# Transposes in lasting PSUM banks, an ordered opening, an output tail in halves, and TensorE in program order through the second attention

## The chip, the cores and the metric

The kernel runs on one core of a Trainium2 chip. The metric is the time of one execution on the device in microseconds (us); the median of several runs is given. Engines are called as in the profile: PE is TensorE's matmuls, PEld its weight loads, DVE VectorE, ACT ScalarE, POOL GpSimd, SP the engine that issues most DMAs.

## The reference

A two-layer encoder step over 2048 prompt frames and 64 sample frames, width 1024, 16 heads of 64, all in float32. Shortened:

```python
# layer 0: chunk-band softmax attention (own chunk of 64 and 8 before it)
q, k, v, gate = split(rms_norm(x, norm_a) @ w_in_a, 4)
p = softmax(q @ k.T * SCALE + rel_bias[clip(rel)] masked to the band)
x = x + ((p @ v) * silu(gate)) @ w_out_a
# keys and values shared by the second layer, from the new x
kb, vb = split(rms_norm(x, norm_kv) @ w_kv, 2)
# layer 1: stick-breaking attention, strictly causal
q, gate = split(rms_norm(x, norm_b) @ w_in_b, 2)
z = q @ kb.T * SCALE
log_fail = where(mask, log_sigmoid(-z), 0)
w = where(mask, exp(log_sigmoid(z) + (sum of log_fail over later keys)), 0)
x = x + ((w @ vb) * silu(gate)) @ w_out_b
y = rms_norm(x, norm_f)
```

The sample frames attend to cached keys as well (512 rows in layer 0, 2048 in layer 1). The outputs are y for both groups and the new rows of keys and values.

## The kernel before

Each float32 factor is kept as two parts, a rounded one (names ending in h) and the rest (ending in l), and a product is the sum of three matmuls (hh, hl, lh). `split` makes the two parts: a copy on ACT, a subtraction on DVE.

There are four stages. **Projections a** (0 to about 727 us): for 17 tiles of 128 frames, `normed` loads a tile (`xt`), takes its squares on ACT (`junk`), the root on POOL (`rstd`), scales it, transposes it on PE into a two-bank PSUM tile (`ps_tr`) and splits it into `x_own` or `big`; values are projected (`ps_v`) with weights `vwh`/`vwl`, made block by block from `vraw` in two halves of the columns. Then keys, queries and gates are projected by `jobs` (`ps_t`) with weights `wh`/`wl`, with `stages` between them that rearrange caches. **First attention** (to about 1323 us), with its output projection (`ps_o`) until 1431 us. **Projections b** (to 2040 us) is the same code on the new x. **Second attention** follows (scores from 2059 to 3201 us), and its last output tiles until 3307 us.

[...] Before, each stage opens its own PSUM pool: in the projections five banks `mm`, two `tr`, one `nat`; in the first attention four for scores `z`, one for sums `acc`, three `wt`; in the second two `z`, two `acc`, one constant (`own`) and three `wt`. The `wt` banks take the transposes of weights and also the accumulation of projections that run beside the attention (`ps_j`, deferred projections, and `ps_o`).

An attention is a list of beats, written out by `Beat`. In the second attention a beat takes one tile of 128 queries against one chunk of up to 512 keys: two score matmuls; f is the sigmoid on ACT; `two` multiplies pairs on POOL; a scan on DVE over `two`; POOL fills the odd places (`s`). On the diagonal (chunk of the queries themselves) the scan takes f directly and widths are 128, 256, 384 and 512. A pack of four tiles' weights is transposed later (`turn`: four 128x128 transposes into a `wt` bank, then the split into `ph` on ACT and `pl` on DVE), and two beats (HOLD) after that multiplied with the values (`products`: sums `acc<-ph,vt` and `acc<-pl,vt`). LAG is the number of beats from an item's last scores to its first `turn`. Heads come in 8 pairs; the frames in two parts (groups of 512 queries 1, 0, then 3, 2), and each pair ends with two or three beats of the sample (`qs`). Key and value chunks have four buffers each. Beside this, `step` takes two of a projection's eight depth blocks (six matmuls) at a rate of 0.3 a beat. `end` drains what is left.

The order of instructions on each engine is chosen at build time: the builder schedules the program by its own timing model, except for instructions that are told to keep the program's order. `InOrder` marks these: in the version before only steps wrapped by `in_place` (loads and splits of projections beside the attention), once `order.amid` is set. On the chip each engine runs its list in order and waits on semaphores.

The output tile (`out_tile`) loads the gated result (`og`) and the residual (`xr`), splits the first into `oh`/`ol` (two buffers each), does 48 matmuls in two halves of columns (the sample's 32), and adds. `finish` then calls `done_b`: squares of 1024 columns on ACT, `rstd` on POOL, one scaling on DVE with the norm's weights `gf`, one DMA. The sample's tile is the last.

Of the kernel before, what the change touches and what calls it, by code (L numbers as in the profile page):

```python
# [9 lines left out]
F32 = mybir.dt.float32  # L10
# [34 lines left out]
LAG = dict(a=2, b=5)  # L45
# [28 lines left out]
class InOrder:  # L74


    def __init__(self, tc):

        self.tc, self.on, self.amid = tc, False, False

    def engine(self, engine):
        outer = self

        class Engine:
            def __getattr__(self, name):
                op = getattr(engine, name)

                def traced(*args, **kwargs):
                    ins = op(*args, **kwargs)  # L89
# [10 lines left out]
def encoder_step(ctx: ExitStack, tc: tile.TileContext, a: dict, o: dict):  # L100
    nc = tc.nc
    order = InOrder(tc)
    dve, act, gps, pe = (order.engine(x) for x in (nc.vector, nc.scalar, nc.gpsimd, nc.tensor))
# [21 lines left out]
    opool = ctx.enter_context(tc.tile_pool(name="out", bufs=1))  # L125

# [79 lines left out]
    def projections(L, x_of, begin, w_v, cv, gv, out_v, jobs, first, prompt, sample, stages):  # L206
        with (
# [7 lines left out]
            with tc.tile_pool(name=f"v_{L}", bufs=2) as pool:  # L215
# [3 lines left out]
                def normed(t, scale=gps.tensor_scalar):  # L219
                    r0, n = TOK[t]  # L220
                    xt = pool.tile([P, D], F32, name="xt", tag="xt", bufs=3)
# [14 lines left out]

                seq = [t for gs_ in ORDER for g in gs_ for t in range(4 * g, 4 * g + 4)] + [len(TOK) - 1]
                if L == "a":
                    seq.sort()
                normed(seq[0], dve.tensor_scalar)  # L240
                begin()
                for half in range(2):
                    wh, wl = [], []
                    for k in range(NK):
                        raw = pool.tile([P, CH], F32, name="vraw", tag="vraw", bufs=2)
                        c = cv + half * CH
                        nc.sync.dma_start(raw, w_v[k * P : (k + 1) * P, c : c + CH])
                        h_ = pool.tile([P, CH], F32R, name="vwh", tag=f"vwh{k}", bufs=1)
                        l_ = pool.tile([P, CH], F32R, name="vwl", tag=f"vwl{k}", bufs=1)
                        act.activation(h_, raw, AF.Copy, scale=gv[:, k : k + 1])  # L250
                        dve.scalar_tensor_tensor(
                            l_, raw, gv[:, k : k + 1], f32(h_), ALU.mult, ALU.subtract
                        )
                        wh.append(h_)
                        wl.append(l_)
                    for i, t in enumerate(seq):
                        r0, n = TOK[t]
                        if half == 0 and i + 1 < len(TOK):
                            normed(seq[i + 1])
# [29 lines left out]
                        if dst is not None:  # L289
                            vn = pool.tile([P, CH], F32, name="vn", tag="vn", bufs=2)  # L290
                            act.activation(vn[:n], out, AF.Copy)
# [6 lines left out]
            with tc.tile_pool(name=f"st_{L}", bufs=5) as spool, tc.tile_pool(name=f"t_{L}", bufs=2) as pool:  # L298
                for j, (kind, w, c0, g) in enumerate(jobs):
                    for hp in range(HP):  # L300
                        for _ in range(-(-len(stages) // (len(jobs) * HP - j * HP - hp))):
                            stages.pop(0)(pool, psum)
# [4 lines left out]
                        nc.scalar.dma_start(raw, w[:, c : c + P].rearrange("(k p) c -> p k c", p=P))  # L307
                        wh = opool.tile([P, NK, P], F32R, name="wh", tag="oh", bufs=2)
                        wl = opool.tile([P, NK, P], F32R, name="wl", tag="ol", bufs=2)
                        scaled_split(wh, wl, raw, g)  # L310
                        for hf, (r0, n, chunks) in enumerate(HALVES):
# [27 lines left out]
                            if kind == "k":  # L339

                                cols = slice(hp * P, hp * P + P)
                                for c in range(0, HALF, CH):
                                    b = hf * HALF + c - first
                                    if b >= 0:
# [3 lines left out]
                                        natural(pool, psum, kf, 0, P, 4, prompt[b : b + CH, cols])  # L348
                                if hf == 0:
# [3 lines left out]
                                    natural(pool, psum, kf, 0, NS, 1, sample[:, cols])  # L353
# [3 lines left out]
    def stage_cache(L, hp, c, pool, psum):  # L357
# [4 lines left out]
        ps = psum.tile([P, CH], F32, name="ps_c", tag="tr", bufs=1)  # L362
# [21 lines left out]
    def stage_diff(where, t, half, pool, psum):  # L384
# [28 lines left out]
    def stage_bias(hp, pool, psum):  # L413
# [13 lines left out]
    def natural(pool, psum, kf, at, n, nt, dst):  # L427
        ps = psum.tile([P, 4, P], F32, name="ps_n", tag="nat", bufs=1)
# [124 lines left out]
    def weigh(pool, psum, acc, blocks, first, last, along=None):  # L553
# [4 lines left out]
        def turn():  # L558
            if along:
                along()  # L560
            wt = psum.tile([P, CH], F32, name="wt", tag="wt", bufs=banks["wt"])
# [26 lines left out]
    def weigh_sample(pool, psum, acc, blocks, first, last):  # L588
# [3 lines left out]
        def turn():  # L592
            wt = psum.tile([P, CH], F32, name="wt", tag="wt", bufs=banks["wt"])
# [51 lines left out]
    def job_steps(L, jobs, x2, psum, first, prompt):  # L645

        return [
            late_job(L, *job, hp, x2, psum, first, prompt)
# [5 lines left out]
    def late_job(L, kind, w, c0, g, hp, x2, psum, first, prompt):  # L654
# [13 lines left out]
        def some(c, k0):  # L668
            if k0 == 0:
                st["ps"] = psum.tile([P, CH], F32, name="ps_j", tag=banks["fo"], bufs=banks[banks["fo"]])  # L670
# [29 lines left out]
        def token_rows(c):  # L700
            kn = st["kn"]
            ps = psum.tile([P, CH], F32, name="ps_r", tag=banks["fo"], bufs=banks[banks["fo"]])
# [42 lines left out]
    def out_steps(L, g, psum, w, residual, done):  # L745

        return [
            out_tile(L, g, t, r0 - g * CH, n, psum, w, residual, done)
# [4 lines left out]
    def out_tile(L, g, t, c0, n, psum, w, residual, done):  # L753
# [17 lines left out]
        def some(c, k0):  # L771
# [3 lines left out]
            if k0 == 0:  # L775
                st["ps"] = psum.tile([P, CH], F32, name="ps_o", tag=banks["fo"], bufs=banks[banks["fo"]])
# [20 lines left out]
        def finish():  # L797
            done(t, n, st["xr"])
# [623 lines left out]
```

## Time and profile before

| | |
|---|---|
| median of 3 runs | 3326.24 us (3325.57 to 3326.41) |
| the profiled execution | 3318.66 us, span 3316.9 us |
| PE busy | 3214.8 us (97%), 17928 matmuls |
| PEld busy | 2795.3 us (84%) |
| DVE, ACT, POOL busy | 1916.7, 1723.0, 1282.8 us |
| mean granted clock of PE | 0.992 |
| DMA | 644.35 MB, mean 194 GB/s |

Busy time of PE is not PE at its peak: a matmul's end is modelled and overlaps the next one, so the time that a dense run of matmuls needs is read from a dense stretch, not from the busy column. A wait is given with the engine that waited, what it was about to do, and the instruction that released it. The granted clock is the share of full speed that PE was allowed.

### The profile page before, as it was taken

How to read it: one execution, taken by the hardware profiler on the slowest of the kernel's cores; microseconds unless marked ns; L12 is line 12 of the kernel's file. 1: busy time of each engine (PE TensorE's matmuls, PEld its weight loads, DVE VectorE, ACT ScalarE, POOL GpSimd, SP SyncE). 2: the span in 40 equal slices, each digit the busy share in tenths (PEclk: the TensorE clock that was granted, in tenths of full speed). 3: DMA queues.
4: the chain of work that ended last, by engine and by line, in shares of the span. 5: the costliest groups of instructions: out<-in, count | busy, mean ns of one | idle time of the engine just before them, and what ended most of it. 6: DMA issues, size and time to landing. Idle time of an engine off the chain costs nothing.

```text
span 3316.9 us, 53520 instructions
## 1 busy us (share of the span) xinstructions
PE 3214.8 (97%) x17928; PEld 2795.3 (84%) x17928; DVE 1916.7 (58%) x3831; ACT 1723.0 (52%) x3730; POOL 1282.8 (39%) x1933
## 2 busy tenths in 40 slices
PE   8999999999899999999999999999999989999998
PEld 7889999988788898878889998888877878888777
DVE  3324431117787776322034333999988888888873
ACT  5323322227897777233134433666766666666651
POOL 2001120005575544011043200444467776777760
PEclk9999999999999999999999999999999999999999
DMA  5449994258889894634399857677635564355523
GB/s 185 147 172 359 344 336 143 92 186 245 237 244 254 230 250 134 200 127 140 111 349 351 292 185 224 193 199 201 188 101 133 158 186 125 122 142 141 134 87 121
DMA packets 457065, 644.35 MB, mean 194 GB/s; under 512 B 49829, under 2 KB 272069, under 8 KB 456790
## 3 DMA queue, kind: packets, MB, share of 16 engines
q1 hardware_dynamic: 397334, 589.80, 57.6%
q10 hardware_dynamic: 59456, 51.13, 4.8%
q8 instruction: 143, 2.34, 0.3%
q14 instruction: 132, 1.08, 0.1%
HBM read 389.90 MB, written 250.90 MB: 193 GB/s over the span
## 4 chain that ended last, share of the span: by engine, by line
PE 81%; DVE 8%; ACT 4%; DMA 4%; issue 2%; POOL 1%; SPq 0%; POOLq 0%; ACTq 0%; DVEq 0%
PE ps_t L89 25%; PE ps_v L89 11%; PE ps_o L89 11%; PE acc L89 10%; PE z L89 8%; PE wt L89 8%; PE ps_j L89 6%; DVE s L89 3%; DVE pl L89 3%; PE ps_tr L89 1%; ACT ph L89 1%; ACT s L89 1%; DVE lwl L89 1%; DMA q<-q_a 1%; PE ps_n L89 0%
## 5 line engine op out<-in xcount | busy, mean ns | idle before, releaser
L89 DVE TENSOR_TENSOR pl<-wt,ph 128x512 fp32r<-128x512 f32 (+1 forms) x864 | 551.5, 654 | 106.2 <-ACT ph L89 103.2
L89 ACT ACTIVATE ph<-wt 128x512 fp32r<-128x512 f32 (+1 forms) x864 | 483.9, 577 | 201.4 <-PE wt L89 193.0
L89 PE MATMUL ps_t<-x_own,wh 128*128 128x362 f32 (+1 forms) x2304 | 570.2, 328 | 0.0
L89 PE MATMUL wt<-ident,s 128*128 128x128 f32 x3472 | 551.6, 275 | 12.5 <-DVE pl L89 9.0
L89 PEld LDWEIGHTS wt<-ident,s 128*128 128x128 f32 x3472 | 420.7, 141 | 87.9 <-DVE pl L89 15.1
L89 ACT ACTIVATE f<-z 128x512 f32<-128x512 f32 (+4 forms) x680 | 355.4, 536 | 185.3 <-PE z L89 122.2
L89 POOL TENSOR_TENSOR s<-f,s 128x256 f32<-128x256 f32 x416 | 360.6, 868 | 133.6 <-DVE s L89 126.3
L89 PEld LDWEIGHTS ps_t<-x_own,wh 128*128 128x128 f32 x2304 | 404.8, 188 | 1.9
L89 PE MATMUL acc<-ph,vt 128*128 128x512 f32 (+3 forms) x1088 | 376.1, 380 | 9.9 <-ACT ph L89 6.7
L89 PE MATMUL z<-kt,q 128*128 128x512 f32 (+3 forms) x1280 | 372.0, 380 | 10.0 <-ACT f L89 8.1
L89 PE MATMUL acc<-pl,vt 128*128 128x512 f32 (+3 forms) x1088 | 364.1, 368 | 17.4 <-DVE pl L89 16.6
L89 PE MATMUL ps_t<-x_own,wl 128*128 128x362 f32 (+1 forms) x1152 | 377.2, 327 | 0.0
L89 POOL TENSOR_SCALAR s<-s,rc 128x640 f32<-128x640 f32 (+5 forms) x264 | 195.9, 749 | 424.2 <-DMA keys<-k_a 250.5
L89 PE MATMUL ps_o<-big,oh 128*128 128x512 f32 x1088 | 336.9, 393 | 4.4 <-ACT oh L89 4.4
L89 DVE TENSOR_TENSOR_SCAN s<-two,s,own 128x256 f32<-128x256 f32 x408 | 299.2, 737 | 35.9 <-POOL two L89 31.7
L89 POOL TENSOR_TENSOR two<-f 128x256 f32<-128x256 f32 x416 | 262.2, 633 | 135.8 <-ACT f L89 117.9
L89 PE MATMUL ps_t<-big,wh 128*128 128x512 f32 x896 | 278.5, 391 | 0.0
L89 PEld LDWEIGHTS z<-kt,q 128*128 128x128 f32 x1280 | 221.7, 191 | 40.9 <-ACT f L89 16.9
L89 PEld LDWEIGHTS ps_o<-big,oh 128*128 128x128 f32 x1088 | 202.7, 188 | 46.7 <-ACT oh L89 5.8
L89 PEld LDWEIGHTS acc<-pl,vt 128*128 128x128 f32 x1088 | 195.2, 191 | 53.1 <-DVE pl L89 38.1
L89 PEld LDWEIGHTS acc<-ph,vt 128*128 128x128 f32 x1088 | 198.0, 191 | 34.6 <-ACT ph L89 13.2
L89 PEld LDWEIGHTS ps_t<-x_own,wl 128*128 128x128 f32 x1152 | 216.3, 188 | 0.1
(146 smaller groups left out, 5536.3 us busy)
## 6 DMA issues: line engine op xcount, KB each, us to landing
vt<-v_b SPq DMA_DIRECT2D x80, 512.0 KB, 4.8
v_b<-vs SPq DMA_DIRECT2D x64, 512.0 KB, 4.8
q<-q_a SPq DMA_DIRECT2D x128, 256.0 KB, 5.8
q<-q_b SPq DMA_DIRECT2D x128, 256.0 KB, 4.2
vt<-v_a SPq DMA_DIRECT2D x48, 512.0 KB, 7.5
kt<-k_b SPq DMA_DIRECT2D x96, 256.0 KB, 6.6
keys<-k_a SPq DMA_DIRECT2D x80, 256.0 KB, 6.0
v_a<-vs ACTq DMA_DIRECT2D x32, 512.0 KB, 2.9
```

Source lines behind the costliest of these rows:

```text
L89: ins = op(*args, **kwargs)
```

## The change

Five things change.

1. A PSUM pool `turned` of three banks (tag `wt`) lives through the whole program. All transposes and the projections beside the attentions take their banks there (`bank`). The projections' own pool has only the five `mm` banks.
2. The opening of both projection stages: `normed` becomes `turned` (load, norm, transposes in two banks) and `parted` (split by halves); x tiles are made two ahead; value weights come as four loads of two blocks into buffers tagged `oh`/`ol`; the first tile, the second tile and the first four loads stand in the program's order on all engines; the first two jobs' weights on ACT's queue wait for the first copy of value rows in the second half of the columns.
3. `finish` is called for each half of the columns, and `done_b` works by halves. Each half's squares are taken as soon as it is added up, and the norm's weights are multiplied before the scaling, which is shared between ACT and POOL.
4. The sample's output tile goes ahead of the last one, and `end` runs one step a beat.
5. PE keeps the program's order in the second attention from the first item on, and LAG there is 6 instead of 5.

```diff
-LAG = dict(a=2, b=5)
+LAG = dict(a=2, b=6)
...
-                    if outer.on:
+                    if outer.on or (outer.stage and outer.stage in whole):
                         outer.tc.keep_in_program_order(ins)
...
-    dve, act, gps, pe = (order.engine(x) for x in (nc.vector, nc.scalar, nc.gpsimd, nc.tensor))
+    dve, act, gps = (order.engine(x) for x in (nc.vector, nc.scalar, nc.gpsimd))
+    pe = order.engine(nc.tensor, ("b",))
...
+    turned_ps = ctx.enter_context(tc.tile_pool(name="turned", bufs=1, space=PSUM))
+
+    def bank(name):
+        return turned_ps.tile([P, CH], F32, name=name, tag="wt", bufs=3)
...
-                def normed(t, scale=gps.tensor_scalar):
+                def turned(t, scale=gps.tensor_scalar):
...
-                    ps = psum.tile([P, NK, P], F32, name="ps_tr", tag="tr", bufs=1)
-                    for k in range(NK):
-                        flip(ps[:, k, :n], xt[:n, k * P : (k + 1) * P])
+                    halves = []
+                    for k0 in range(0, NK, 4):
+                        ps = bank("ps_tr").rearrange("p (k t) -> p k t", k=4)
+                        for k in range(4):
+                            flip(ps[:, k, :n], xt[:n, (k0 + k) * P : (k0 + k + 1) * P])
+                        halves.append(ps[:, :, :n])
+                    return halves
+
+                def parted(t, halves):
...
-                    split(*(x[:, :, c : c + n] for x in xs[hf]), ps[:, :, :n])
+                    for k0, ps in zip(range(0, NK, 4), halves):
+                        split(*(x[:, k0 : k0 + 4, c : c + n] for x in xs[hf]), ps)
...
+                def two_blocks(half, j):
+                    raw = opool.tile([P, 2, CH], F32, name="vraw", tag=("oh", "ol")[j % 2], bufs=2)
+                    c = cv + half * CH
+                    src = w_v[2 * j * P : (2 * j + 2) * P, c : c + CH]
+                    nc.sync.dma_start(raw, src.rearrange("(k p) c -> p k c", p=P))
+                    for i in range(2):
...
+                        act.activation(h_, raw[:, i], AF.Copy, scale=gv[:, k : k + 1])
+                        dve.scalar_tensor_tensor(l_, raw[:, i], gv[:, k : k + 1], f32(h_), ALU.mult, ALU.subtract)
...
-                normed(seq[0], dve.tensor_scalar)
-                begin()
...
+                    if half == 0:
+                        order.on = True
+                        tile0 = turned(seq[0], dve.tensor_scalar)
+                        begin()
+                        two_blocks(0, 0)
+                        parted(seq[0], tile0)
+                        two_blocks(0, 1)
+                        tile1 = turned(seq[1])
+                        two_blocks(0, 2)
+                        parted(seq[1], tile1)
+                        two_blocks(0, 3)
+                        order.on = False
+                    else:
+                        for j in range(NK // 2):
+                            two_blocks(1, j)
...
-                        if half == 0 and i + 1 < len(TOK):
-                            normed(seq[i + 1])
+                        if half == 0 and i + 2 < len(TOK):
+                            parted(seq[i + 2], turned(seq[i + 2]))
...
+                        with tc.issue_after(first_copy.ins) if j == 0 and hp < 2 else nullcontext():
+                            nc.scalar.dma_start(raw, w[:, c : c + P].rearrange("(k p) c -> p k c", p=P))
+                            scaled_split(wh, wl, raw, g)
...
         def end(self):
+            self.rate = 1.0
...
-            order.amid = False
+            order.amid, order.stage = False, None
...
         def summed(g):
-            beat.beside += out_steps("b", g, psum, w_out, x1_rows, done_b)
+            at = -1 if g == GROUPS and len(beat.beside) > 1 else len(beat.beside)
+            beat.beside[at:at] = out_steps("b", g, w_out, x1_rows, done_b)
...
-        return [in_place(x) for x in [load] + cuts], products, [[partial(out, 0)], [partial(out, CH), finish]]
+        return [in_place(x) for x in [load] + cuts], products, [[partial(out, c), partial(finish, c)] for c in range(0, D, CH)]
...
-        def done_b(t, n, xr):
-            junk = pool.tile([P, D], mybir.dt.bfloat16, name="junk", tag="junk", bufs=1)
-            r = rstd_of(pool, xr, n, junk)
-            dve.scalar_tensor_tensor(xr[:n], xr[:n], r[:n], gf[:n], ALU.mult, ALU.mult)
+        def done_b(t, n, xr, c):
+            i, half = c // CH, xr[:n, c : c + CH]
...
+            act.activation(junk[:n], half, AF.Square, scale=D**-0.5, accum_out=ss[:n, i : i + 1])
+            if i:
...
+                dve.tensor_scalar(ms[:n], ss[:n, 0:1], ss[:n, 1:2], EPS, ALU.add, ALU.add)
...
+                gps.tensor_tensor(r[:n], ms[:n], nhalf[:n], ALU.pow)
+            dve.tensor_tensor(half, half, gf[:n, c : c + CH], ALU.mult)
+            if i == 0:
+                return
...
-            nc.sync.dma_start(dst, xr[:n])
+            act.activation(xr[:n, :CH], xr[:n, :CH], AF.Copy, scale=r[:n])
+            gps.tensor_scalar(xr[:n, CH:], xr[:n, CH:], r[:n], 1.0, ALU.mult, ALU.mult)
+            for x in range(0, D, CH):
+                nc.sync.dma_start(dst[:, x : x + CH], xr[:n, x : x + CH])
...
         beat.lead(LEAD["b"])
+        order.stage = "b"
         beat.item(*first)
```

More of the change, by code (lines that the diff above doesn't have):

```diff
@@ L551, in gate_steps, with weigh @@
         return [shift, close]
-    def weigh(pool, psum, acc, blocks, first, last, along=None):
+    def weigh(pool, acc, blocks, first, last, along=None):
         st = {}
@@ L560, in turn @@
                 along()
-            wt = psum.tile([P, CH], F32, name="wt", tag="wt", bufs=banks["wt"])
+            wt = bank("wt")
             n = 0
@@ L586, in weigh, with weigh_sample @@
         return turn, products
-    def weigh_sample(pool, psum, acc, blocks, first, last):
+    def weigh_sample(pool, acc, blocks, first, last):
         st = {}
         def turn():
-            wt = psum.tile([P, CH], F32, name="wt", tag="wt", bufs=banks["wt"])
+            wt = bank("wt")
             n = len(blocks())
@@ L669, in some @@
             if k0 == 0:
-                st["ps"] = psum.tile([P, CH], F32, name="ps_j", tag=banks["fo"], bufs=banks[banks["fo"]])
+                st["ps"] = bank("ps_j")
             ps, wh, wl = st["ps"], st["wh"], st["wl"]
@@ L701, in token_rows @@
             kn = st["kn"]
-            ps = psum.tile([P, CH], F32, name="ps_r", tag=banks["fo"], bufs=banks[banks["fo"]])
+            ps = bank("ps_r")
             for j in range(4):
@@ L775, in some @@
             if k0 == 0:
-                st["ps"] = psum.tile([P, CH], F32, name="ps_o", tag=banks["fo"], bufs=banks[banks["fo"]])
+                st["ps"] = bank("ps_o")
             ps = st["ps"] if n == NS else st["ps"][:n]
@@ L1131, in encoder_step @@
         beat.lead(LEAD["a"])
+        order.stage = "a"
         beat.item(*first)
@@ L1191, in turn @@
             def turn():
-                ps = psum.tile([P, CH], F32, name="ps_e", tag="wt", bufs=banks["wt"])
+                ps = bank("ps_e")
                 for j in range(HP):
@@ L1318, in pack @@
                 along = gt if h and c == 0 and i == 0 else None
[L1319 removed]
+                return *weigh(lpool, acc, lambda: [block(j) for j in packs[i]], first, last, along), done
             return [partial(tile_of, t) for t in range(4)], [pack(i) for i in range(len(packs))]
```

101 lines of the change are left out of this document (52 added, 49 removed).

## The prediction

> **What bounds the kernel now.** I read the busy times by stage first, then the groups of matmuls and the waits inside the second attention, then the timeline at both ends and where two stages meet. In the table of stretches the columns are the time, then PE, PEld, DVE, ACT and POOL busy (with counts), the granted clock, the DMA share and GB/s.
>
> ```profile
> 0.00:25.00 25.00, 13.99 (x58) 10.95 (x59) 10.34 (x16) 16.39 (x29) 8.44 (x16) 1.00 0.74 220
> 1425.00:1447.00 22.00, 18.37 (x81) 14.58 (x80) 5.59 (x9) 7.66 (x15) 3.08 (x4) 0.84 0.26 83
> 2059.00:2387.00 328.00, 317.62 (x1860) 269.77 (x1859) 293.81 (x506) 220.53 (x501) 146.76 (x250) 0.99 0.72 200
> 2387.00:3205.00 818.00, 787.15 (x4444) 648.36 (x4443) 694.92 (x1127) 544.47 (x1095) 592.49 (x1086) 0.99 0.48 135
> 3205.00:3308.00 103.00, 101.84 (x472) 83.65 (x470) 41.88 (x68) 24.04 (x47) 11.41 (x18) 1.00 0.37 126
> 3308.00:3317.00 9.00, 0.00 (x0) 0.00 (x0) 2.79 (x4) 1.34 (x3) 0.54 (x1) 0.69 0.13 29
> ```
>
> PE is busy nearly everywhere, so only its gaps are for sale. The gaps that the change touches: the opening (11 of 25 us), the meeting of the first attention with the second projections (3.6 of 22 us), the second attention (2059 to 3205), and the last 9 us. The busy column hides stalls, because matmuls overlap. The chain that ended last gives the dense spacing:
>
> ```profile
> 3223.58 84.00 PE ps_o L89 x368
> 100.30 0.87 PE ps_tr L89 x8
> ```
>
> A matmul of 512 columns costs 84.00/368 = 0.228 us, a transpose 0.87/8 = 0.109 us. The second attention has these (window 2059 to 3205):
>
> ```profile
> L89 PE MATMUL z<-kt,q 128*128 128x512 f32 (+3 forms) x1280 | 372.0, 380 | 10.0 <-ACT f L89 8.1 <-DMA kt<-k_b 1.5
> L89 PE MATMUL wt<-ident,s 128*128 128x128 f32 x2284 | 369.5, 275 | 6.4 <-DVE pl L89 3.6 <-DVE pp L89 1.3 <-POOL s L89 1.1
> L89 PE MATMUL acc<-ph,vt 128*128 128x512 f32 (+1 forms) x634 | 246.7, 407 | 0.5 <-ACT ph L89 0.2
> L89 PE MATMUL acc<-pl,vt 128*128 128x512 f32 (+1 forms) x634 | 238.6, 393 | 16.4 <-DVE pl L89 16.0
> L89 PE MATMUL ps_j<-big,lwh 128*128 128x512 f32 x466 | 149.0, 395 | 0.3 <-DVE pl L89 0.2
> L89 PE MATMUL ps_j<-big,lwl 128*128 128x512 f32 x234 | 92.5, 395 | 0.0
> L89 PE MATMUL ps_o<-big,oh 128*128 128x512 f32 x263 | 84.8, 397 | 0.8 <-ACT oh L89 0.8
> L89 PE MATMUL ps_o<-big,ol 128*128 128x512 f32 x131 | 52.0, 397 | 0.0
> ```
>
> By the loops, scores and sums come to 384 full beats and 64 triangular groups worth 2.5 beats each: 544 beats of two scores and two sums, 2176 matmuls of 512 columns, 496 us. Transposes: 2284 x 0.109 = 249 us. Projections beside them: (466+234+263+131) x 0.228 = 249 us. The sample's scores and sums add about 50 us (120 and 248 matmuls by the loops, the latter of 128 columns, taken as a transpose each). Dense, the stage is 1044 us; it takes 1146. The stall is 102 us, against the 41 us that the busy column leaves (1146 - 317.62 - 787.15). [...]
>
> What the weight loads, which wait first, were held by:
>
> ```profile
> PEld acc L89 <- DVE pl L89: 40.8, 62, 5.0
> PEld z L89 <- ACT f L89: 17.2, 28, 3.6
> PEld wt L89 <- DVE pl L89: 5.9, 9, 1.4
> ```
>
> The largest item is a sum (acc) that stands too close behind the split (pl, on DVE) of its own transposed weights.
>
> **The change, part by part.** The sum is made against the profiled execution, 3318.66 us (span 3316.9 and 1.8 around it); the median of the runs is 3326.24, 0.23% higher, and I take the same microseconds off it. A measurement tells about 0.2% (6.7 us) from no change.
>
> *Opening.* These are ACT's rows, and PE's first value matmul:
>
> ```profile
> 7.03 2.45 ACT L89 ACTIVATE wh<-wraw,g_a 128x128 fp32r<-128x128 f32 x8 [1.37 <-DMA g_a<-in_norm_a]
> 9.38 1.32 ACT L89 ACTIVATE vwh<-vraw,g_a 128x512 fp32r<-128x512 f32 x2
> ...
> 11.76 1.02 ACT L89 ACTIVATE x_own<-ps_tr 128x1024 fp32r<-128x1024 f32 x1
> 12.84 0.79 PE L89 MATMUL ps_v<-vwh,x_own 128*128 128x512 f32 x1 [3.48 <-ACT x_own L89]
> ```
>
> The early split of a later job's weights (wh, 2.45 us) leaves this place. Its DMA, on ACT's queue, and its split now stand behind the first copy of rows in the second half, the thirteenth of seventeen tiles here; four tiles of 24 matmuls are still to come (22 us) for a load and those 2.45 us, so nobody waits. In the second projections that copy is the half's first. And the tile's split goes ahead of the next tile's square, so the first value matmul comes near 9.1 instead of 12.84. The value weights arrive as four DMAs of two blocks, all issued at once, instead of eight through two buffers. From 9 to 17 us ACT's eight vwh (0.66 each), four half splits and two squares become the pace. I take 4 us; between 0 (ACT the pace throughout) and 7.
>
> *Lasting banks.* At two meetings PE waited for banks of the closing stage:
>
> ```profile
> PE ps_tr L89 <- issue: 2.3, 1, 2.3
> PE ps_v L89 <- ACT x_own L89: 1.2, 1, 1.2
> PE ps_j L89 <- DVE sl L89: 2.2, 1, 2.2
> PE ps_j L89 <- ACT sg L89: 1.6, 1, 1.6
> ```
>
> The last two (2040 and 727 us, where deferred products begin) go, since the product takes a bank that the projections' last results do not hold: 2.2 and 1.6 us; at worst the weights of the deferred job come no sooner, and nothing is gained. The first two (1431 to 1437) are also followed by a clock of 0.84 over 22 us, 3.5 us lost. The flips of two tiles no longer wait. Late next are the value weights: they now land in the output projection's own buffers (tags oh, ol), and the last two of the four can only be loaded when the last output tile's matmuls end. By the opening's rows a load and two splits cost some 5 us from there; 12 products of the first tile (2.8 us) cover part. So about 3 us of idle remain of 5.5, and the clock is partly saved: I take 3.7, between -1 (idle as long as now, clock no better) and 9. [...]
>
> Transposes of tiles, cached keys and rows of keys now share three banks, with no row that shows a cost: 0, between -1 and +2. At the end of the first attention PE waits once for an output tile's split:
>
> ```profile
> 1326.14 1.20 PE L89 MATMUL ps_o<-big,oh 128*128 128x512 f32 x4 [2.52 <-ACT oh L89]
> ```
>
> With the drain at one step a beat this falls elsewhere; it may vanish or come back at the next tile, so I take 1 us, between 0 and 2.5. The sample's output tile, moved ahead of the last one, moves its two loads on SP's queue too, by one tile; 11 us of the matmuls of a tile (48 x 0.228) hide them.
>
> *Second attention.* No instruction is removed on PE. The order becomes the program's: in a beat the transposes of one pack, then two scores, then the two sums of the pack turned two beats ago, then a share of projection. Beats are 1146/680 = 1.69 us (680 by the loops), so a sum has 3.4 us from its transposes. What must happen in them (all rows of the transposed banks in this window):
>
> ```profile
> L89 ACT ACTIVATE ph<-wt x572: 371/599/657, 2068.4 to 3203.6; 128x512 fp32r<-128x512 f32 x168, 128x256 fp32r<-128x256 f32 x23
> L89 DVE TENSOR_TENSOR pl<-wt,ph x572: 388/668/694, 2069.4 to 3204.9; 128x512 fp32r<-128x512 f32 x168, 128x256 fp32r<-128x256 f32 x23
> ```
>
> 0.60 + 0.67 = 1.27 us of work, and DVE is busy 90% in the first stretch (293.81/328) and 85% in the second, so one or two other DVE instructions stand ahead: about 2.5 us. That fits into 3.4, so most of the 40.8 us goes. It does not all turn into time: DVE at 90% cannot give the first 328 us more than some 20, and the next wait is the bank. Three banks serve the transposes, one of them held by a projection, so pack n needs pack n-2 split when it starts, 2.9 us after the flips: just enough. I take half of 40.8 + 5.9, 23 us. Scores wait for f as now (17.2). PE executes the compiled order in any case; the builder's timing model could fill the place ahead of a score whose keys are late, the program's order does not: in the second part each head pair's first keys get their buffer only when the pair before has made its last scores, three sample beats (5 us) ahead, and
>
> ```profile
> kt<-k_b SPq DMA_DIRECT2D x96, 256.0 KB, 6.6
> ```
>
> so up to 1.6 us more at seven places, and up to 1 us behind SP's queue: I charge 3 of 11. Two half-clock stretches (0.99 of 328 and of 818, together up to 11 us by rounding, 7 by two windows like that of 1431) may lose one: 3. One more beat of lag lies in the drain, under output tiles: 0. Net 23, between 66 (all of the three rows and the clock's 3) and -38 (the bank's case below).
>
> *Tail.*
>
> ```profile
> 3308.23 0.68 DVE L89 TENSOR_TENSOR ol<-ol,xr 64x512 f32<-64x512 f32 x1 [2.17 <-ACT ol L89]
> 3309.01 0.68 DVE L89 TENSOR_TENSOR xr<-ps_o,ol 64x512 f32<-64x512 f32 x1
> 3309.78 1.06 ACT L89 ACTIVATE junk<-xr 64x1024 bf16<-64x1024 f32 x1 [1.58 <-DVE xr L89]
> ...
> 3311.83 1.28 DVE L89 SCALAR_TENSOR_TENSOR xr<-xr,rstd,gf 64x1024 f32<-64x1024 f32 x1 [0.72 <-POOL rstd L89]
> 3313.13 0.51 SPq L1216 DMA_DIRECT2D out_y_s<-xr  x1
> ```
>
> The last tile is now a prompt tile: one addition instead of two and a copy (1.5 us less between PE's end and the square), a square of 512 instead of 1024 (0.4 less), a scaling of two halves on ACT and POOL instead of 1.28 (0.6 less), one DMA issue more (0.5 more): 2.0, between 1 and 3. The extra halves add to ACT and POOL 0.6 us a tile each, under PE (second attention: ACT 67%, POOL 64%).
>
> Sum: 4 + 2.2 + 1.6 + 3.7 + 1 + 23 + 2 = 37.5. Forecast 3326.2 - 37.5 = 3289; for the profiled execution 3318.7 - 37.5 = 3281.
>
> **Rivals.**
> *Same order, same stalls.* If the compiled order is already near the program's, or DVE sets the pace, the attention keeps its 102 us and only 14.5 us come: 3312 (3305 to 3322). For it: DVE's 90%. Against: 62 waits of sums in the rows.
> *The bank decides: slower.* Each of some 640 packs that finds no bank stops PE, with its scores, sums and projections queued behind, and behind these f on ACT and the split on DVE. The price is 640 times the wait added; beyond 14.5/640 = 0.023 us a pack over what the sums save, the kernel is slower. At 0.06 us it costs 38: 3326 - 14.5 + 38 = 3350. For it: the 5.9 us of wt waiting for pl already there, with 2.9 us for 2.5. Against: only 9 such waits in 1146 us.
> *All waits go.* The three rows (64 us) vanish: 3326 - 14.5 - 62 = 3250. Against: DVE's share.
> *The clock.* In-order waits that break PE's stream more often could lower the granted clock more often. A dip like that of 1431 costs 3.5 us, so eleven more would eat the forecast: 3326. The 0.99 of both rows, with 102 us of stalls already in them, speaks against it. [...]
>
> **How the numbers follow.** Forecast 0.52 (its own range 3265 to 3308), same stalls 0.20, the bank 0.15, all waits gone 0.10, the clock 0.03. The range 3243 to 3332 leaves out most of the bank's case and a little below. Slower: most of the bank's: 0.14. Within 0.2%: 0.06, from the edges of three cases. Faster: 0.80.
>
> **What would show it.** First value matmul near 9 us; no PE wait at 2040; a gap at 1431 that waits for a value weight's DMA; in the second attention acc waiting for pl well under 40.8 and wt for pl above 5.9; the stage near 1120 us; no more than 8 us after PE's last matmul. Wrong if the stage is not under 1140, or if wt or z take over what acc loses.

## The result and the profile after

| | before | after |
|---|---|---|
| median (lowest to highest), us | 3326.32 (3325.57 to 3327.66), 4 runs | 3308.18 (3299.12 to 3313.78), 4 runs |
| ratio, 95% interval | 1 | 0.9941 (0.9924 to 0.9959) |
| profiled execution, its span, us | 3318.66, 3316.9 | 3308.37, 3306.6 |
| mean granted clock | 0.992 | 0.992 |

The change takes 18.1 us off, about half of the 37.5 forecast. The time lies inside the range, and next to the rival "same order, same stalls" (3312). The two profiled executions differ by only 10.3 us, because the one before is 7.7 us below the median of its kernel. The traces can place these 10.3 us; where the other 7.8 lie, no trace here shows.

First, the kernel after by stretches (columns as in the prediction's first table):

```profile
0.00:25.00 25.00, 17.26 (x77) 13.93 (x78) 12.94 (x23) 17.60 (x30) 9.32 (x18) 1.00 0.82 274
1421.00:1443.00 22.00, 19.32 (x88) 14.80 (x87) 11.63 (x20) 11.07 (x20) 5.64 (x7) 0.92 0.63 200
2052.00:2380.00 328.00, 311.53 (x1825) 263.87 (x1823) 290.98 (x501) 218.75 (x496) 146.78 (x248) 0.99 0.70 198
2380.00:3188.00 808.00, 781.22 (x4456) 651.52 (x4454) 706.05 (x1133) 554.00 (x1118) 598.42 (x1090) 0.99 0.49 138
3188.00:3299.00 111.00, 107.13 (x491) 88.14 (x492) 48.27 (x84) 35.84 (x79) 22.84 (x31) 0.98 0.38 119
3299.00:3307.00 8.00, 0.42 (x2) 0.00 (x0) 1.50 (x3) 1.44 (x3) 1.61 (x2) 0.81 0.17 66
```

PE does 77 matmuls in the first 25 us instead of 58, the meeting of the stages has a clock of 0.92 instead of 0.84, and the end is 8 us instead of 9. The two windows of the second attention are 10 us shorter in sum, but the window behind them, up to the last matmuls, is 8 us longer (111 against 103), so that hardly anything is left. What held the weight loads in the second attention (2052 to 3200):

```profile
PEld wt L89 <- DVE pl L89: 22.4, 39, 1.9
PEld z L89 <- ACT f L89: 17.0, 21, 2.8
PEld wt L89 <- POOL two L89: 8.2, 8, 1.7
PEld wt L89 <- issue: 6.6, 12, 1.7
PEld ps_o L89 <- ACT oh L89: 5.5, 2, 3.6
PEld ps_o L89 <- DVE ol L89: 4.9, 2, 3.8
...
PEld acc L89 <- DVE pl L89: 3.0, 5, 1.3
```

Sums waiting for their split fell from 40.8 to 3.0 us. Transposes waiting for a bank, for the same split on DVE, rose from 5.9 to 22.4, and the smaller rows (pairs on POOL, issue, an output tile's split) take most of the rest. All rows of this view together come to 85.7 us before (2059 to 3205) and 75.9 after.

To place the time, the span is cut at marks that each kernel's trace has: PE's first value matmul, the last projection of the first stage, the first score of the first attention, its last, the first transpose of the second projections, the first score of the second attention, the last matmul, the end. Durations in us, in the profiled execution of each; e1 and e2 are the change without its order, with six and five beats of lag (experiments 1 and 2):

| stretch | before | after | e1 | e2 |
|---|---|---|---|---|
| to the first value matmul | 12.8 | 9.0 | 9.2 | 9.2 |
| projections a | 714.3 | 714.6 | 715.1 | 714.8 |
| to the first score | 11.7 | 9.7 | 9.8 | 9.7 |
| first attention, scores | 560.5 | 567.3 | 562.7 | 561.5 |
| its drain and output tiles | 134.7 | 132.0 | 132.0 | 132.0 |
| projections b | 625.6 | 619.5 | 619.2 | 618.6 |
| second attention to the last matmul | 1247.6 | 1246.9 | 1248.6 | 1245.0 |
| to the end | 9.7 | 7.6 | 7.6 | 7.6 |

The stretches outside the attentions give 16.4 us in the kernel after (16.9 in e2) where the forecast had 14.5. The second attention gives 0.7 instead of 23, and the scores of the first cost 6.8. Each column is one execution.

### The profile page after: what moved, and what is told of

Same layout as the page of the kernel before. It is cut to its first block, busy times and chain, and to the rows that moved or that the text cites. A ratio compares the mean times of both kernels' runs of the same rounds, so it can differ in the third digit from the quotient of the medians.

```text
span 3306.6 us, 53618 instructions
## 1 busy us (share of the span) xinstructions
PE 3206.2 (97%) x17928; PEld 2797.8 (85%) x17928; DVE 1937.2 (59%) x3882; ACT 1738.6 (53%) x3815; POOL 1300.3 (39%) x1950
## 4 chain that ended last, share of the span: by engine, by line
PE 80%; DVE 5%; DMA 5%; issue 5%; ACT 3%; POOL 2%; SPq 1%; POOLq 0%; ACTq 0%; DVEq 0%
PE ps_t L89 26%; PE ps_v L89 11%; PE acc L89 10%; PE z L89 10%; PE wt L89 9%; PE ps_o L89 8%; PE ps_j L89 5%; DVE s L89 2%; DVE pl L89 2%; ACT ph L89 1%; PE ps_tr L89 1%; ACT s L89 1%; DMA q<-q_a 1%; DVE lwl L89 1%; PE ps_c L89 1%
## 5 line engine op out<-in xcount | busy, mean ns | idle before, releaser
L89 ACT ACTIVATE ph<-wt 128x512 fp32r<-128x512 f32 (+1 forms) x864 | 492.1, 576 | 336.7 <-PE wt L89 325.4
L89 DVE TENSOR_TENSOR pl<-wt,ph 128x512 fp32r<-128x512 f32 (+1 forms) x864 | 560.2, 655 | 135.0 <-ACT ph L89 130.3
L89 PE MATMUL wt<-ident,s 128*128 128x128 f32 x3472 | 536.6, 275 | 30.2 <-DVE pl L89 22.9
L89 PE MATMUL z<-kt,q 128*128 128x512 f32 (+3 forms) x1280 | 411.0, 403 | 11.8 <-ACT f L89 9.5
L89 PE MATMUL acc<-ph,vt 128*128 128x512 f32 (+3 forms) x1088 | 352.1, 357 | 9.5 <-ACT ph L89 6.3
L89 PE MATMUL acc<-pl,vt 128*128 128x512 f32 (+3 forms) x1088 | 348.5, 354 | 2.3 <-DVE pl L89 2.2
L89 DVE TENSOR_TENSOR_SCAN s<-two,s,own 128x256 f32<-128x256 f32 x408 | 299.4, 737 | 27.8 <-POOL two L89 24.5
L89 PEld LDWEIGHTS z<-kt,q 128*128 128x128 f32 x1280 | 198.7, 192 | 23.4 <-ACT f L89 16.7
```

## The experiments

Each kernel was timed in five rounds beside the kernel before (medians 3325.74 for experiments 1 to 4, 3327.52 for 5 to 8, 3326.96 for 9 to 12). "Ratio" is to the kernel before, with its 95% interval; the kernel after stands at 0.9941 (0.9924 to 0.9959).

**1 and 2. All of the change but the order.** The builder orders PE again; the second also takes the lag back to 5.

```diff
-    pe = order.engine(nc.tensor, ("b",))
+    pe = order.engine(nc.tensor)
-LAG = dict(a=2, b=6)        # e2 only
+LAG = dict(a=2, b=5)
```

> The changed kernel with PE left to the builder's order in the second attention (lag 6 kept). If the program's order is worth nothing as it stands (its saved sum waits of 38 us come back as waits for a bank and for splits), this is within 5 us of the changed kernel: 3302 to 3313 us, with acc waiting for pl back near 40 us in the weight loads and wt for pl back near 6. If the order gains and something else of the change lost the time, this is 15 us or more slower than the changed kernel (3323 or more). If the order loses, it is faster than 3300.

> The same with lag 5 as before: only lasting banks, opening, drain and tail are left of the change. By milestones of the two traces (second attention starts 7.5 us earlier, tail 2 us shorter) I expect 3326 - 10 to 18 = 3308 to 3316 us whichever theory of the order holds; if it is near 3326, the order and the lag carry the gain; if under 3303, they cost.

Measured: e1 3310.18, 0.9952 (0.9939 to 0.9965); e2 3305.29, 0.9938 (0.9925 to 0.9950). Without the order the time is the same within the intervals, so the gain belongs to the other four parts. (e2 is 3 us below the range that I had named.) The weight loads' waits of e1 and then of e2 in the second attention:

```profile
PEld acc L89 <- DVE pl L89: 38.6, 66, 1.9
PEld z L89 <- ACT f L89: 17.5, 28, 5.7
...
PEld wt L89 <- DVE pl L89: 6.0, 10, 1.2
```

```profile
PEld acc L89 <- DVE pl L89: 40.9, 62, 4.9
PEld z L89 <- ACT f L89: 14.6, 24, 4.2
PEld wt L89 <- DVE pl L89: 5.0, 8, 1.4
```

These are close to the waits of before (40.8, 17.2, 5.9). So the program's order did what it was said to do to the sums, and a different set of waits of about the same length came with it.

**3. The order with five beats of lag.** One line: `LAG = dict(a=2, b=5)`.

> The changed kernel with PE in program order and lag 5. If the chain from scores to weights (f, two, scan, s) is what the sixth beat covers, wt waits for POOL's s more often and the time rises by 5 to 20 us over the changed kernel (3313 to 3328). If the waits are for the bank only, the lag does not matter: 3303 to 3313.

Measured: 3325.41, 0.9995 (0.9984 to 1.0006): 17 us slower than with six beats. The waits:

```profile
PEld wt L89 <- DVE pl L89: 26.6, 48, 1.2
PEld wt L89 <- POOL s L89: 16.7, 20, 1.8
```

With the order fixed, transposes come before POOL has filled in their weights (`s`: 16.7 us, 1.8 in the kernel after). The sixth beat pays for the order; it is no gain beside it (e1 against e2: the builder's order has no use for it). In this trace the second attention is 18.3 us longer than in the kernel after, and some 10 us of that are a lower clock (see the clock rival below).

**4. The order and the sixth beat in the kernel before.**

```diff
-LAG = dict(a=2, b=5)
+LAG = dict(a=2, b=6)
...
-    dve, act, gps, pe = (order.engine(x) for x in (nc.vector, nc.scalar, nc.gpsimd, nc.tensor))
+    dve, act, gps = (order.engine(x) for x in (nc.vector, nc.scalar, nc.gpsimd))
+    pe = order.engine(nc.tensor, ("b",))
...
```

> The kernel before with only TensorE in program order through the second attention and lag 6. If the order gains nothing because waits for a bank replace waits for a split, 3320 to 3332 us, with acc waiting for pl under 5 us and wt for pl over 15 in the weight loads. If my forecast of the order was right and the rest of the change lost the time, 3296 to 3310. If the order costs, above 3333.

Measured: 3329.98, 1.0010 (1.0002 to 1.0019). Alone, this part is a loss of 3 to 4 us, by the interval 0.7 to 6.3. Its waits move as in the kernel after:

```profile
PEld wt L89 <- DVE pl L89: 21.7, 37, 1.9
...
PEld acc L89 <- DVE pl L89: 5.6, 9, 1.3
```

**5 and 6. Is the fourth bank what is missing?** `own`, a constant, holds a PSUM bank through the second attention. Experiment 5 puts it in SBUF; experiment 6 gives the free bank to the projections beside the attention, so that all three `wt` banks serve the transposes.

```diff
-        own = psum.tile([P, CH], F32, name="own")
+        own = wpool.tile([P, CH], F32, name="own")
...
+        # e6 only, in bank():
+        if beside_ps[0] is not None and name in ("ps_j", "ps_r", "ps_o", "ps_e"):
+            return beside_ps[0].tile([P, CH], F32, name=name, tag="fo", bufs=1)
...
```

> The changed kernel with the scan's constant second operand (own) kept in SBUF instead of its PSUM bank; that bank stays empty. It is the control of the next run. No theory expects more than a different scan time: 3303 to 3313 us, with the scan of 256 at 0.74 us as before; if reading SBUF makes DVE's scan slower or faster by 0.05 us, 408 scans give 20 us of DVE time and, where DVE sets the pace, up to 10 us.

> As the control, and the freed bank takes the projections beside the second attention (until the drain), so that transposes have all three lasting banks. If the bank is what ate the gain, wt waiting for pl falls from 22 us to under 8 and the time is 10 to 25 us under the control (3283 to 3298). If DVE sets the pace, the wait moves on (to z waiting for f, or to DVE's own queue) and the time stays within 5 us of the control. If the single bank of the projections stalls PE instead, ps_j waits for the evacuation and it is slower.

Measured: e5 3445.61, 1.0357 (1.0343 to 1.0370); e6 3428.11, 1.0303 (1.0290 to 1.0316). I had not reckoned with the move itself, which costs 137 us. The scan reads `own`. Its row in the kernel after, then in e5 (count | busy us, mean ns of one | idle before):

```profile
L89 DVE TENSOR_TENSOR_SCAN s<-two,s,own 128x256 f32<-128x256 f32 x408 | 299.4, 737 | 27.8 <-POOL two L89 24.5 <-PE wt L89 2.2
```

```profile
L89 DVE TENSOR_TENSOR_SCAN s<-two,s,own 128x256 f32<-128x256 f32 x407 | 421.2, 1038 | 50.2 <-POOL two L89 48.7
```

0.30 us more for each, on an engine that was 89% busy at the start of the stage. That spoils experiment 5 as a test of banks, but e6 against e5 still is one, with a slow DVE in both. Weight-load waits of e5, then of e6:

```profile
PEld wt L89 <- DVE pl L89: 100.6, 102, 3.7
PEld z L89 <- ACT f L89: 31.5, 34, 2.8
PEld acc L89 <- DVE pl L89: 22.7, 31, 1.8
```

```profile
PEld acc L89 <- DVE pl L89: 89.4, 103, 2.7
PEld z L89 <- ACT f L89: 40.4, 45, 2.2
...
PEld wt L89 <- DVE pl L89: 8.8, 9, 1.3
```

The bank does take the transposes' wait away (100.6 to 8.8), and of these 92 us, 67 come back at the sums and 9 at the scores (31.5 to 40.4): 17.5 us net by the medians. With DVE slow, PE waits for `pl` wherever it meets it first. Whether a fourth bank would pay at the usual speed of the scan was not tried.

**7. Output tiles' splits later.** In the second attention, the first matmuls of an output tile wait twice, for `oh` and `ol` (5.5 and 4.9 us). Experiment 7 gives them, and the first matmuls of every other projection beside this attention, seven beats more.

```diff
-                    self.ready = self.clock + 9
+                    self.ready = self.clock + (16 if order.stage == 'b' else 9)
```

> The changed kernel with the first product of a newly begun projection in the second attention held back for 16 beats after its load instead of 9. In the trace the first output tile's products stand at the head of PE's list while its split is late: 3.4 and 3.5 us near 2722, then 6.8 us at half clock. If in-order waiting there costs what the trace shows, this saves 5 to 10 us: 3298 to 3303. If the wait only comes back elsewhere, within 3 us of the changed kernel.

Measured: 3304.41 (3296.6 to 3308.6), 0.9930 (0.9918 to 0.9942). The interval overlaps that of the kernel after, and the waits that it was to remove are still there (4.8 us for `oh`, 4.2 for `ol`). The long one for `oh` ends at 2726 us in both traces. So the edit did not move them, and what they are worth stays open.

**8. Sums three beats behind the transposes instead of two.** One line: `HOLD = dict(a=1, b=3)`.

> The changed kernel with sums three beats behind the transposes instead of two. If the sums already have time enough (acc waits for pl only 3 us in the weight loads), nothing is gained: within 4 us of the changed kernel. If the bank decides, nothing changes either, since a bank is free when it is split and not when it is summed. Only if sums were still late would it be 5 us or more faster.

Measured: 3321.0 (3315.4 to 3328.4), 0.9981 (0.9973 to 0.9990): 13 us slower than the kernel after, against what I expected. New rows appear, and `wt` behind `pl` stays at 22.5 us in 2050 to 3210; what ties them to the longer hold stays open.

```profile
PEld wt L89 <- DVE pp L89: 11.0, 14, 1.8
PEld wt L89 <- POOL s L89: 9.3, 12, 1.2
```

**9 and 10. Less work on DVE, the computation whole.** The small halves of the weights of the projections beside the attention (`lwl`, 112 times 0.51 us on DVE) are made on POOL. Experiment 9 keeps the order, 10 leaves it to the builder with five beats of lag.

```diff
-            scaled_split(st["wh"][:, ks], st["wl"][:, ks], st["raw"][:, ks], g[:, ks])
+            if L == "a":
+                scaled_split(st["wh"][:, ks], st["wl"][:, ks], st["raw"][:, ks], g[:, ks])
+                return
+            raw = st["raw"]
+            for k in range(k0, k0 + STEP):
+                act.activation(st["wh"][:, k], raw[:, k], AF.Copy, scale=g[:, k : k + 1])
+                gps.tensor_scalar(raw[:, k], raw[:, k], g[:, k : k + 1], 1.0, ALU.mult, ALU.mult)
+            gps.tensor_tensor(st["wl"][:, ks], raw[:, ks], f32(st["wh"][:, ks]), ALU.subtract)
```

> The changed kernel with the rest parts of the deferred projections' weights (lwl, 112 of about 0.5 us on DVE) made on POOL instead. It takes 53 us of DVE's work out of the first 640 us of the second attention and touches neither banks nor the order. If DVE being late is what every one of these waits comes down to, a third to two thirds of it turns into time: 3273 to 3292 us. If the number of banks or PE's order decides and DVE's load does not, within 5 us of the changed kernel (3303 to 3313). If POOL, then near 80% busy, is late instead, wt waits for s and it is slower.

> The same move, with PE in the builder's order and lag 5. If the order is worth nothing either way, as far from its own base (3305) as the run before is from the changed kernel: 3270 to 3290 when DVE decides, 3300 to 3310 when not. If the program's order only pays once DVE is less late, this one gains less than the run before by 5 us or more.

Measured: e9 3300.48 (3298.7 to 3305.5), 0.9922 (0.9908 to 0.9936); e10 3301.4 (3298.1 to 3303.3), 0.9922 (0.9908 to 0.9935). These are the best whole kernels run here, lower than the kernel after by 7 us in the median, with intervals that overlap its own. e9 falls between the two ranges that I had named (3273 to 3292 if DVE's lateness is behind every wait, 3303 to 3313 if it does not matter); e10 lies in its range for DVE not deciding. Order or not, again, makes no difference. The waits of e9, then of e10:

```profile
PEld z L89 <- ACT f L89: 21.1, 29, 2.8
PEld wt L89 <- DVE pl L89: 16.6, 31, 1.0
```

```profile
PEld acc L89 <- DVE pl L89: 27.8, 52, 1.6
PEld z L89 <- ACT f L89: 21.4, 31, 7.3
```

The wait for `pl` falls in both, whichever instruction it stands at: from 23.4 (after, in the same window) to 16.6, and from 40.9 (e2) to 27.8. Scores waiting for `f` take part of it back: 17.0 to 21.1 in e9, and 14.6 to 21.4 in e10.

**11 and 12. How much DVE can give.** Every second pack's rest `pl` is left out in the second attention, the rounded part being used twice, so PE and ACT do the same work and DVE less: 857.9 us busy between 2050 and 3190 in experiment 11, 999.0 in the kernel after. Experiment 11 keeps the order, 12 does not; both have six beats of lag.

```diff
+            banks["n"] = banks.get("n", 0) + 1
+            if order.stage == "b" and banks["n"] % 2:
+                act.activation(st[0][:, :n], wt[:, :n], AF.Copy)
+                st[1] = st[0]
+                return
```

> The changed kernel, where every second pack of the second attention leaves out the rest part of its weights (pl; the sum takes ph twice instead). PE's work is the same; DVE loses some 290 of its pl (about 190 us), and a bank of such a pack is free after ACT alone. If DVE's lateness is the stage's limit, the second attention falls from 1135 us towards the dense 1044 plus waits for f: 40 to 80 us, 3228 to 3268. If PE's order or other waits hold it, less than 15 us is gained (3293 or more).

> The same omission with PE in the builder's order, lag 6. If the order is worth nothing by itself, within 6 us of the run before. If the program's order is what lets PE use a faster split (my forecast's reason, hidden so far by DVE), 10 us or more slower than the run before. If the builder's order, made for the actual durations, uses it better, faster.

Measured: e11 3289.06 (3287.4 to 3291.8), 0.9888 (0.9871 to 0.9904); e12 3294.97 (3292.7 to 3296.4), 0.9903 (0.9889 to 0.9918). The waits of e11, then of e12:

```profile
PEld z L89 <- ACT f L89: 16.2, 22, 3.1
PEld wt L89 <- DVE pl L89: 7.6, 15, 1.0
```

```profile
PEld z L89 <- ACT f L89: 23.3, 38, 5.9
PEld acc L89 <- ACT ph L89: 8.5, 29, 0.8
PEld acc L89 <- DVE pl L89: 6.6, 11, 1.3
```

Half of the packs have no `pl` to wait for, and their banks are free after ACT alone, so shorter rows alone would prove little; the time falls as well, by 19 us against the kernel after and by 15 against e1. That is under the 40 to 80 us that I had named for DVE as the stage's limit. Here the order is the better one by 5.9 us between medians. The runs of the two do not overlap, their intervals do, and I had named 6 us as no difference; of the 10.7 us between the second attentions of the two traces, 3.4 are a lower clock (mean over the span 0.992 and 0.991). Even in e11 the second attention keeps 1229.1 us (after: 1246.9), so DVE is not the only limit. Scores waiting for `f` (two `z` banks) stay at 10.9 us (e3) or more in every kernel, and no run here took them away.

## Why the prediction was right or wrong

- **Opening: right.** Forecast first value matmul near 9.1 us and 4 us saved; measured 8.96, and 3.5 us net of projections a (3.9 less 0.4). The split of `vwh` and the first copy of rows have changed places with the early weights; ACT's rows and PE's first value matmul, after:

```profile
6.84 1.33 ACT L89 ACTIVATE vwh<-vraw,g_a 128x512 fp32r<-128x512 f32 x2 [1.43 <-DMA vraw<-in_w_in_a]
8.30 0.60 ACT L89 ACTIVATE x_own<-ps_tr 128x512 fp32r<-128x512 f32 x1
...
8.96 0.79 PE L89 MATMUL ps_v<-vwh,x_own 128*128 128x512 f32 x1
```

- **Banks at 727 and 2040: right.** Neither wait is in the trace after. Way to the first score 2.0 us shorter (forecast 1.6); the 2.2 at 2040 lies in the 6.1 us by which projections b are shorter.
- **Meeting at 1431: size near, mechanism wrong.** Forecast 3.7, with a gap that waits for a value weight's DMA. Idle in 22 us fell from 3.63 to 2.68 and the clock rose from 0.84 to 0.92: 1.0 and 1.8 us, 2.8 together. The wait of `ps_v` at 1437 (1.2) is what went; the gap itself is as long as before, and what PE waits for in it is the first tile's norm. After, in order of time (PE's wait last):

```profile
1419.88 1.04 ACT L89 ACTIVATE junk<-xt 128x1024 bf16<-128x1024 f32 x1
...
1430.26 0.69 DVE L89 TENSOR_TENSOR xr<-ps_o,xr 128x512 f32<-128x512 f32 x1 [4.75 <-PE ps_o L89]
1430.87 0.14 DVE L89 TENSOR_SCALAR ms<-ss 128x1 f32<-128x1 f32 x1
1431.14 0.56 POOL L89 TENSOR_TENSOR rstd<-ms,nhalf 128x1 f32<-128x1 f32 x1 [97.35 <-DVE ms L89]
1431.73 0.75 DVE L89 TENSOR_SCALAR xt<-xt,rstd 128x1024 f32<-128x1024 f32 x1 [0.72 <-POOL rstd L89]
```

```profile
PE ps_tr L89 <- issue: 2.4, 1, 2.4
```

  The squares are done at 1420.9, but `ms` on DVE stands in the program's order behind the last output tile's addition (`xr`, to 1430.9) and starts ten microseconds later. The weights were there in time. In the kernel before, without an ordered opening, the same `ms` ran at 1334.7, and its gap of 2.3 us ended when the last bank of the closing stage had been read (addition to `xr` until 1433.75, transposes from 1433.96). An ordered opening has this price: it also holds what was ready early.

  The granted clock was 0.50 for 6.8 us from 1434.1 before, and for 3.4 us from 1433.4 after, behind gaps of about the same length, 2.3 and 2.4 us. So the gaps do not tell why the clock was low for half as long after; that less idle would save part of the loss was an estimate. Of the 3.5 us lost to the clock half came back (1.8). The prediction also counted 5.5 us of idle where its own table leaves 3.6 (22 - 18.37).
- **Drain of the first attention: right in itself.** Forecast 1 of at most 2.5; its wait at 1326 is gone (0.3 us left), and the stretch is 2.7 us shorter. The first attention's scores took 6.8 us more, which I had at nothing. One of its waits grew from 2.1 us (first row) before to 6.2 (second) after:

```profile
PE ps_r L89 <- POOL lkn L89: 2.1, 1, 2.1
```

```profile
PE ps_r L89 <- POOL lkn L89: 6.2, 1, 6.2
```

  In all kernels with lasting banks this wait is 3.8 us or more, in the two with the banks of before 2.1 and 2.0 (e4), so some 2 to 4 us go with the banks. The rest need not: e1 and e2 have the same first attention as the kernel after and take 562.7 and 561.5, and the twelve traces with lasting banks run from 561.5 to 569.0, against 560.5 and 561.9 without. Why the same program varies so much stays open.
- **Second attention: wrong, and this is the step that failed.** "I take half of 40.8 + 5.9, 23 us." The working before it held: a sum now has its 3.4 us, and `acc` behind `pl` fell to 3.0. The prediction had also named the next wait, the bank, and written that wt or z taking over would make it wrong. It then valued what remains of the two waits at half, with nothing but the two ends to go by. The rows show that the microseconds went from one form to another: 40.8 to 3.0 at the sums, 5.9 to 22.4 at the banks, and 8.2, 6.6, 5.5 and 4.9 in rows that had been smaller. Of 23 us, 0.7 came in the traces. In them the time from the first score to the last did fall, from 1141.5 to 1135.4 us, but the time from there to the last matmul rose from 106.1 to 111.5 for about as many matmuls (491 and 492); the prediction had put the longer lag in the drain at nothing. Against the medians of e1 and e2 the order gains 2.0 us or loses 2.9, which the intervals do not tell from nothing. The two small terms beside the 23 (3 for late keys, 3 for the clock) cancel in the sum; the trace after has 0.6 us of scores waiting for keys and 1.7 us more lost to the clock.

  What the runs put in its place: the split on DVE is late for whoever asks first (100.6 us at the banks in e5, 89.4 at the sums in e6; 16.6 at the banks in e9, 27.8 at the sums in e10), and the order chooses who asks. That the waits change places and the time stays is shown by e1, e2 and e4. That DVE's load is the reason is shown in part: with less work on DVE the waits and the time do fall (e9 to e12), by a part of what they would if it were the only one. DVE at 89 to 90% of the first 328 us, which the prediction quoted as the reason for the rival "same order, same stalls", was the better guide than the 62 waits that spoke against it. That rival's reason is only half right too: the compiled order is not near the program's, and DVE alone does not set the pace (e11 keeps 1229.1 us of 1246.9).
- **Bank rival: half right.** Its place was right, its price was not: some 39 waits of 0.6 us, no 640 waits of a constant. With five beats of lag (e3) a loss does come, 17 us, but partly at POOL's `s` and partly by the clock.
- **Clock rival:** no sign of it in the kernel after. Mean clock 0.992 in both. Stretches with a granted clock of 0.50 in the second attention add up to 17 us before and 20.5 after, half of which, by an estimate from the 0.50, is lost. In e3, where `wt` waits longer (26.6 us for `pl` and 16.7 for `s`, against 23.4 and 1.8), the mean clock is 0.990, the half-clock stretches reach 41 us, and half of the 20 us more is some 10 us lost; whether the waits cause that was not tested.
- **Tail: right.** Forecast 2.0 us and no more than 8 after the last matmul; measured 2.1 and 7.6. The square, the root and the scaling, after:

```profile
3300.24 0.63 ACT L89 ACTIVATE junk<-xr 128x512 bf16<-128x512 f32 x1 [4.67 <-DVE xr L89]
...
3301.29 0.92 POOL L89 TENSOR_TENSOR rstd<-ms,nhalf 128x1 f32<-128x1 f32 x1 [7.77 <-DVE ms L89]
3302.25 0.72 ACT L89 ACTIVATE xr<-xr,rstd 128x512 f32<-128x512 f32 x1 [1.29 <-POOL rstd L89]
```

So the direction and the six small terms held, near enough, and one term of 23 us did not come. In the traces the forecast is 27 us too large: 22 in the second attention and 7 in the first, less 2 that the other stretches gave beyond their terms. In the medians it is 19 too large. That the time lies inside the range says little, since the range was 89 us wide; the gain came without the step that made up most of the forecast.

## What to carry to other kernels

In these traces a wait in a row named the place where a late result was first asked for. Before giving a reordering credit for such a row, look at how busy the engine is that makes the result: at 90%, as here, the wait mostly turned up at the next instruction that asked (40.8 to 3.0 us at the sums, 5.9 to 22.4 at the banks), and the row's size was the ceiling of the gain and not its estimate. Waits at stage meetings, at the opening and in the tail, where DVE is busy for 10.34 of 25, 5.59 of 22 and 2.79 of 9 us, did return what their rows promised (16.4 us for 14.5).

## What the hardware showed that I had not expected

- **Where a constant lies.** The scan whose second operand lies in SBUF instead of PSUM (e5) takes 1.04 us instead of 0.74 on average. In the view of one tile (least/median/most in ns, 2400 to 3180 us), after and then e5:

```profile
L89 DVE TENSOR_TENSOR_SCAN s<-two,s,own x325: 715/737/750, 2401.4 to 3179.3; 128x256 f32<-128x256 f32 x163
```

```profile
L89 DVE TENSOR_TENSOR_SCAN s<-two,s,own x280: 717/1077/1641, 2399.3 to 3177.9; 128x256 f32<-128x256 f32 x140
```

  The fastest one is as fast as before (717 against 715), half of them take 0.34 us longer or more, up to 0.9: so the extra time is not the same for every scan. In the same trace POOL's `two` goes from 0.63 to 0.74 us and its copy from 0.20 to 0.39 (means, 2400 to 3180 us). What makes them longer was not tested.
- **Runs of one kernel follow the granted clock, but not it alone.** The four of the kernel after took 3299.12, 3307.98, 3308.37 and 3313.78 us at 0.995, 0.992, 0.992 and 0.991. A thousandth of a span of 3307 us is 3.3 us, so by an estimate the step from 0.995 to 0.991 is worth 13 of the 14.7 us between the ends. But executions of the kernel before with the same clock of 0.992 took from 3318.66 (the profiled one) to 3333.54 us. A difference of 8 us or less between two versions of this kernel needs more executions than one profile of each.
